# Block products of an MLP in another order with early weight differences, and a norm's row scale applied at the up projection's evacuation

## The chip, the cores and the metric

The kernel runs on one core of a Trainium2 chip. A core has a matrix engine (PE) and a vector engine (DVE), a scalar engine (ACT), a general engine (POOL) and an engine that issues most of the transfers (SP). Each runs its own list of instructions in order; they wait for one another by semaphores. The metric is the device time of one execution in microseconds. The kernel before took 896.69 us, the median of 3 runs (895.31 to 898.7).

## The reference, cut to what matters

One layer works on 512 tokens of width 1024: a mixer of recurrent heads, a cross-attention to 256 memory tokens, and a multilayer perceptron (MLP). The change touches the end of the second step and the whole third:

```python
x = x + cross_attention(rmsnorm(x, norm_xattn[l]), rmsnorm(mem, norm_mem[l]),
                        w_xq[l], w_xkv[l], w_xo[l])
x = x + squared_relu_mlp(rmsnorm(x, norm_mlp[l]), w_up[l], w_down[l])
return rmsnorm(x, norm_final)

def rmsnorm(x, g):
    y = x32 * lax.rsqrt(jnp.mean(x32 * x32, axis=-1, keepdims=True) + NORM_EPS)
    return y * g
def squared_relu_mlp(xn, w_up, w_down):
    return jnp.square(jax.nn.relu(xn @ w_up)) @ w_down
```

The factor 1/rms of a token is positive and the same for all of its columns. So relu(r·z) equals r·relu(z), and the factor can be applied before the up product or behind it.

## The kernel before, in words

**A product.** All products are of fp32 precision, made of three matmuls each: an operand is split into a rounded high part and the rest, and high·high, high·low and low·high are added in PSUM (`mm3`, L223 to L226). A weight tile of 128x1024 comes by a transfer into a buffer `st`, ACT rounds it to `wh` (L220), DVE subtracts to get `wl` (L221). There are three buffers each of `st`, `wh` and `wl`, and three weights are prepared ahead of the one in use.

**Stages.** The input projection and the recurrent heads come first (to about 390 us), then the mixer's output projection "out" with the residual addition, the query projection and the cross-attention, its output projection "xo", and from 545 us on the MLP. "out" and "xo" take the output columns in two halves c of 512, each with four tiles of 128 tokens. Behind "out" (`proj_res`) each finished piece is added to the residual, its squares are summed for the norm, and PE transposes it in four 128x128 pieces (`transp`, L768) while the next pieces are still in work; the norm's 1/rms goes into the attention later. Behind "xo" (`proj_res_norm`) nothing is transposed in the first half. In the second half, for each of the four tiles, the two sums of squares are added, POOL raises the mean to the power -1/2 (L166), DVE and ACT multiply the two halves of x by that factor (L788, L789), and only then PE transposes both: eight groups of four transposes, all behind the last matmuls of "xo".

**The MLP.** It has four blocks f of 1024 hidden columns. In a block, the *up stage* makes eight slices (p, j) of 128 hidden columns for all 512 tokens, 24 matmuls each. ACT evacuates a slice with Relu (L964) and squares it (L965); DVE and ACT then form the differences of token halves and split them. The *down stage* multiplies by the block's part of the down matrix with seven block products P1 to P7 in place of eight, each for the two halves g of the hidden columns: 14 jobs of 12 matmuls, 168 in all (L1006 to L1008). The products need differences of weight tiles, for which `source` (L891) issues four DVE subtractions per half g, 128x1024 each. The products gather in three pairs of PSUM banks: X takes P1, then P6, P7 and P4 on top of it; Y takes P2; Z takes P5, then P3. Whenever a bank holds a value that an output piece needs, `add_to` adds it to the residual on DVE (L938), and the next product may write into that bank only after. Behind the last block's adds come the final norm and the output transfers.

**Order.** The code is written stage by stage; a scheduler orders the instructions of each engine by priorities, and the preparation of weights has high priority. At run time each engine follows that order without exception, so what stands behind a waiting instruction waits too.

The jobs' order and the buffers before:

```python
G4 = lambda dt=F32: T("gate", 1024, 3, dt)      # three buffers of 128x1024
ORDER = ("P1", "P2", "P5", "P6", "P3", "P7", "P4")
JOBS = [("P1", 0), ("P2", 0), ("P1", 1), ("P2", 1)] + [(p, g) for p in ORDER[2:] for g in range(2)]
```

Of the kernel before, what the change touches and what calls it, by code (L numbers as in the profile page):

```python
# [18 lines left out]
P = 128  # L19
# [58 lines left out]
def trunk(ctx: ExitStack, tc: tile.TileContext, x, mem, wpk, vec, cst, lmask, rmask, rows, out):  # L78
# [12 lines left out]
    def T(tag, w, bufs, dt=F32):  # L91
        return (sb if w == 516 else big).tile([P, w], dt, tag=tag, name=nm(tag), bufs=bufs)
# [4 lines left out]
    def smb():  # L97
        return pss.tile([P, 512], F32, tag="sm", name=nm("sm"))
# [8 lines left out]
    A16 = lambda: T("as", 2560, 2)  # L107
    A4 = lambda dt=F32: T("a4", 1024, 10, dt)
    T2 = lambda: T("t2", 516, 5)
    G4 = lambda dt=F32: T("gate", 1024, 3, dt)  # L110
    VV = lambda: T("vv", 516, 8)
    XT = lambda: [T("xT", 4096, 2, F32R) for _ in range(2)]
    YT1 = lambda dt=F32R: T("yT", 1024, 8, dt)
# [7 lines left out]
    grow1 = G4()  # L121
# [532 lines left out]
    def gate_proj(c0, bcol, silu):  # L654
        gt = G4()
# [40 lines left out]
    rate[0] = 2  # L696
    mv_proj()
    rate[0] = 1
    mo0 = gate_proj(4096, V_MO, False)
    mo1 = gate_proj(4352, V_MO + 2, False)  # L700

    mt = [A4(), A4()]
# [57 lines left out]
                stats(st, t, c)  # L760
                transp(tgt, t, c)

    def transp(tgt, t, c, src=None):
        dst, gcol = tgt
        src = xr[t, c] if src is None else src
        ps = smb()
        for k in range(4):
            pe.transpose(ps[:, k * P:k * P + P], src[:, k * P:k * P + P], ident)  # L768
        for k in range(4):
            g = vc[:, gcol + 4 * c + k:gcol + 4 * c + k + 1]  # L770
            hi = dst[c][:, k * 1024 + t * P:k * 1024 + t * P + P]
            lo = dst[c][:, k * 1024 + 512 + t * P:k * 1024 + 512 + t * P + P]
            sc.activation(hi, ps[:, k * P:k * P + P], AF.Copy, scale=g)
            v.scalar_tensor_tensor(out=lo, in0=ps[:, k * P:k * P + P], scalar=g, in1=hi.bitcast(F32), op0=ALU.mult, op1=ALU.subtract)  # L774

    def proj_res_norm(mat, src, tgt, st, pre):

        for c in range(2):
            for t, ps in proj_t(mat, 0, 512 * c, src, pre=pre if c == 0 else None, late=c == 1):
                v.tensor_tensor(out=xr[t, c], in0=ps, in1=xr[t, c], op=ALU.add)  # L780
                stats(st, t, c)
                if c == 0:
                    continue
                s1 = tiny(1)
                v.tensor_tensor(out=s1, in0=st[:, 2 * t:2 * t + 1], in1=st[:, 2 * t + 1:2 * t + 2], op=ALU.add)
                r, _ = rstd_of(s1, 1, D)
                n0, n1 = T2()[:, 0:512], T2()[:, 0:512]
                v.tensor_scalar(out=n0, in0=xr[t, 0], scalar1=r, scalar2=None, op0=ALU.mult)  # L788
                sc.activation(n1, xr[t, 1], AF.Copy, scale=r)  # L789
                transp(tgt, t, 0, n0)  # L790
                transp(tgt, t, 1, n1)

    def rstd_tok(st, n=1.0):
        s4 = tiny(4)
# [94 lines left out]
    def source(f, p, g):  # L889
        b11, b12, b21, b22 = [raw[f, 4 * g + n] for n in range(4)]  # L890
        sub = lambda o, a, b: v.tensor_tensor(out=o, in0=a, in1=b, op=ALU.subtract)  # L891
# [59 lines left out]
    for f in range(4):  # L951

        sta = []
        for p in range(4):
            a = []
            for j in range(2):
                ps, = proj_d("up", 1024 * f + P * (p + 4 * j), x3, count=1)
                raw_load(f, 2 * p + j)
                if p == 3 and j == 1:
                    with tc.high_priority():  # L960
                        job(f, 0)
                        job(f, 1)
                y = T2()[:, 0:512]
                sc.activation(y, ps, AF.Relu)  # L964
                sc.activation(y, y, AF.Square)  # L965
                a.append(y)
            if p % 2 == 0:
# [19 lines left out]
            e["P5"], e["P6"] = [(ya[:, u:u + 256], ya[:, 512 + u:768 + u]) for u in (0, 256)]  # L987
            e["P7"], e["P3"] = [(yb[:, u:u + 256], yb[:, 512 + u:768 + u]) for u in (0, 256)]
            sta.append(e)
        fin = f == 3  # L990
        if fin:
            gfin = G4()
# [131 lines left out]
```

## Time and profile before

| what | value |
|---|---|
| median of 3 runs | 896.69 us |
| profiled execution | 896.54 us |
| its span, first to last instruction | 894.8 us |
| mean granted PE clock | 0.991 of full |
| PE busy | 860.9 us, 96% |
| DVE busy | 592.4 us, 66% |
| ACT busy | 434.3 us, 49% |
| up stage of a block (629.40 to 672.90 us) | 43.5 us |
| down stage of a block (588.50 to 629.40 us) | 40.9 us |
| last down stage (841.98 to 886.37 us) | 44.4 us |

All times in the prediction are microseconds from the span's start. In the rows of a timeline stand the start, the duration, the engine, the line and the operation, output and inputs, and in brackets the idle time just before and what ended it. Matmuls overlap: one of 128x512 is listed with 0.39 us, and the next starts 0.227 us after it, so a distance between starts says more than a duration. In a table of windows each engine has its busy time and, in brackets, its instructions, and at the end stand the granted PE clock (1.00 is full), the share of the transfer engines and GB/s.

### The profile page before, as it was taken

The page shows a single profiled execution, that of the slowest core. Times are in us where ns is not written, and L with a number is a line of the kernel's source. Part 1 is how long each engine was busy: PE and PEld are TensorE (multiplying, and loading weights), DVE is VectorE, ACT ScalarE, POOL GpSimd, SP SyncE. Part 2 cuts the span into 40 slices and gives each one's busy share as a digit, 9 for nine tenths or more (in the row PEclk, how much of TensorE's full clock was granted, in tenths as well). Part 3 has the DMA queues.
Part 4 walks back from the last instruction along what each step waited for, and adds up shares of the span by engine and source line. Part 5 has one row for each costly group of instructions (what it writes and reads, how often), then busy time and mean ns, then how long its engine had stood idle before and what let it go on. Part 6 is the DMA issues. An engine that isn't in the chain of part 4 may idle for free.

```text
span 894.8 us, 11089 instructions
## 1 busy us (share of the span) xinstructions
PE 860.9 (96%) x4194; PEld 711.5 (80%) x4194; DVE 592.4 (66%) x1016; ACT 434.3 (49%) x793; POOL 20.4 (2%) x53
## 2 busy tenths in 40 slices
PE   7999999999999999999999998999999999999985
PEld 5887888888876987887888876887887788778864
DVE  5557688689346977654555455688568746955785
ACT  5235443353358567454445355553554356436534
POOL 1000000010010000000000000000000000000000
PEclk9999999999999999999999998999999999999998
DMA  7422222221142333522222422403330432052002
GB/s 255 133 101 73 75 82 77 96 78 54 48 141 71 99 126 107 166 93 94 71 67 76 143 70 71 142 24 117 118 118 25 141 118 94 24 188 95 1 1 94
DMA packets 24615, 84.21 MB, mean 94 GB/s; under 512 B 2865, under 2 KB 2993, under 8 KB 24562
## 3 DMA queue, kind: packets, MB, share of 16 engines
q1 hardware_dynamic: 24272, 83.04, 27.3%
q8 instruction: 33, 0.54, 0.3%
q10 hardware_dynamic: 290, 0.47, 0.2%
q14 instruction: 20, 0.16, 0.1%
HBM read 81.40 MB, written 2.10 MB: 93 GB/s over the span
## 4 chain that ended last, share of the span: by engine, by line
PE 54%; DVE 11%; ACT 3%; issue 2%; POOL 1%; POOLq 0%; ACTq 0%
PE mm L225 13%; PE mm L224 13%; PE mm L226 13%; DVE wl L221 5%; PE sm L1006 2%; PE sm L1007 2%; PE sm L1008 2%; ACT wh L220 2%; PE sm L628 2%; PE sm L613 2%; DVE a L891 2%; DVE vv L938 1%; PE sm L226 1%; PE sm L225 1%; PE sm L224 1%
## 5 line engine op out<-in xcount | busy, mean ns | idle before, releaser
L221 DVE TENSOR_TENSOR wl<-st,wh 128x1024 fp32r<-128x1024 f32 x109 | 133.4, 1224 | 154.1 <-ACT wh L220 150.7
L224 PE MATMUL mm<-xT,wh 128*128 128x512 f32 x552 | 219.6, 399 | 0.1
L225 PE MATMUL mm<-xT,wh 128*128 128x512 f32 x552 | 215.9, 392 | 0.2 <-DVE xT L774 0.2
L226 PE MATMUL mm<-xT,wl 128*128 128x512 f32 x552 | 216.0, 392 | 0.0
L220 ACT ACTIVATE wh<-st 128x1024 fp32r<-128x1024 f32 x109 | 115.3, 1058 | 182.1 <-PE mm L225 83.7
L226 PEld LDWEIGHTS mm<-xT,wl 128*128 128x128 f32 x552 | 103.7, 188 | 22.2 <-issue 0.6
L224 PEld LDWEIGHTS mm<-xT,wh 128*128 128x128 f32 x552 | 103.8, 188 | 21.7 <-issue 1.4
L225 PEld LDWEIGHTS mm<-xT,wh 128*128 128x128 f32 x552 | 103.9, 188 | 21.3 <-DVE xT L774 0.8
L1006 PE MATMUL sm<-wh,yT 128*128 128x512 f32 x128 | 50.3, 398 | 5.4 <-DVE vv L938 5.4
L1007 PE MATMUL sm<-wl,yT 128*128 128x512 f32 x128 | 51.1, 399 | 1.5 <-DVE wl L221 1.5
L224 PE MATMUL mm<-wh,yT 128*128 128x512 f32 x128 | 50.4, 394 | 0.0
L226 PE MATMUL mm<-wh,yT 128*128 128x512 f32 x128 | 50.3, 393 | 0.0
L225 PE MATMUL mm<-wl,yT 128*128 128x512 f32 x128 | 50.0, 391 | 0.0
L1008 PE MATMUL sm<-wh,yT 128*128 128x512 f32 x128 | 48.9, 394 | 0.0
L220 ACT ACTIVATE wh<-as 128x1024 fp32r<-128x1024 f32 x24 | 25.5, 1061 | 40.7 <-PE mm L225 21.4
L221 DVE TENSOR_TENSOR wl<-as,wh 128x1024 fp32r<-128x1024 f32 x24 | 29.4, 1224 | 16.1 <-ACT wh L220 16.1
L938 DVE TENSOR_TENSOR vv<-sm,vv 128x512 f32<-128x512 f32 x48 | 31.7, 685 | 6.4 <-PE sm L1008 6.4
L1006 PEld LDWEIGHTS sm<-wh,yT 128*128 128x128 f32 x128 | 24.3, 190 | 12.0 <-issue 4.3
L220 ACT ACTIVATE wh<-a 128x1024 fp32r<-128x1024 f32 x20 | 20.8, 1058 | 23.6 <-PE sm L1008 23.3
L375 PEld LDWEIGHTS sm<-a,t 128*128 128x128 f32 x224 | 30.2, 192 | 2.2 <-ACT t L365 0.4
L365 ACT ACTIVATE t<-a 128x512 f32<-128x512 f32 x28 | 18.4, 673 | 26.3 <-DVE a L428 24.0
L166 POOL TENSOR_TENSOR tiny<-tiny,misc 128x1 f32<-128x1 f32 (+1 forms) x22 | 16.4, 747 | 641.3 <-DVE tiny L947 334.5
(264 smaller groups left out, 1590.3 us busy)
## 6 DMA issues: line engine op xcount, KB each, us to landing
st<-in_wpk SPq DMA_DIRECT2D x109, 512.0 KB, 3.2
as<-in_wpk SPq DMA_DIRECT2D x16, 512.0 KB, 4.1
gate<-in_wpk SPq DMA_DIRECT2D x8, 512.0 KB, 3.3
a<-in_wpk SPq DMA_DIRECT2D x8, 512.0 KB, 5.1
as<-in_x SPq DMA_DIRECT2D x4, 512.0 KB, 6.4
vv<-in_x SPq DMA_DIRECT2D x8, 256.0 KB, 4.0
out<-vv SPq DMA_DIRECT2D x7, 256.0 KB, 2.2
a<-in_mem SPq DMA_DIRECT2D x2, 512.0 KB, 4.0
```

What stands on the lines that cost most here:

```text
L220: sc.activation(dst_hi, src, AF.Copy)
L221: v.tensor_tensor(out=dst_lo, in0=src, in1=dst_hi.bitcast(F32), op=ALU.subtract)
L224: pe.matmul(ps, lhsT=ah, rhs=bh, start=first, stop=False)
L225: pe.matmul(ps, lhsT=ah, rhs=bl, start=False, stop=False)
L226: pe.matmul(ps, lhsT=al, rhs=bh, start=False, stop=last)
L365: sc.activation(t[:, 0:512].rearrange("p (b e j) -> p b e j", e=2, j=L), ap(k, 0, [2 * L, 512 // (2 * L)], [512 + L, 2], [1, L]), AF.Copy)
L375: pe.matmul(ps[:, z], lhsT=kc[:, z], rhs=ap(q2, w * P, [2 * L, P // (2 * L)], [512 + L, 2], [1, L]), start=True, stop=True)
L613: pe.matmul(ps, lhsT=k[:, ws * P:ws * P + P], rhs=q, start=True, stop=True)
L938: v.tensor_tensor(out=z, in0=ps, in1=z, op=ALU.add)
L1006: pe.matmul(ps, lhsT=ah, rhs=bh, start=new, stop=False, **fl)
L1007: pe.matmul(ps, lhsT=ah, rhs=bl, start=False, stop=False, **fl)
L1008: pe.matmul(ps, lhsT=al, rhs=bh, start=False, stop=end and k == 1, **fl)
```

## The change

There are three parts.

1. **The norm behind "xo".** `proj_res_norm` goes; "xo" uses `proj_res` as "out" does, so that the unscaled x is transposed piece by piece. The factor 1/rms of all 512 tokens is computed once, on 128x4 numbers. PE turns it into a row (four transposes of a column spread over 128 columns, `rms_row`), and ACT copies it to `rrow`, which holds each token's factor in every partition. Each up slice's evacuation multiplies by it: ACT's Relu becomes a DVE instruction, max(ps, 0)·rrow (L964), and ACT squares as before.
2. **The products.** ORDER becomes P1, P2, P6, P5, P7, P3, P4. The differences b22-b12 and T2 = b22-b12+b11 are formed in `early_sums`, called behind the second and the fourth pair of up slices; P6 then takes T2 and P7 takes b12 as they are, and P5 and P4 keep one subtraction each. The number of subtractions stays at eight per block. The raw down weights are requested in the first six slices of a block's up stage, two at once in the first two, where before one was requested in each of the eight.
3. **Buffers.** The three `gate` buffers become two and one named `rg` of the same size, which holds in turn a gain row, a gate, `rrow` and the final gain row.

```diff
-    G4 = lambda dt=F32: T("gate", 1024, 3, dt)
+    G4 = lambda dt=F32: T("gate", 1024, 2, dt)
+    RG = lambda: T("rg", 1024, 1)
...
-    proj_res_norm("xo", os_, (x3T, V_MLP), st2, drain)
+    proj_res("xo", 0, os_, (x3T, V_MLP), st2, drain)
     x3 = xk(x3T)
+    ms2 = rstd_tok(st2)
+    r4 = tiny(4)
+    gp.tensor_tensor(out=r4, in0=ms2, in1=nh.to_broadcast([P, 4]), op=ALU.pow)
+    rrow = RG()
+
+    def rms_row():
+        ps = smb()
+        for t in range(4):
+            pe.transpose(ps[:, t * P:t * P + P], r4[:, t:t + 1].to_broadcast([P, P]), ident)
+        sc.activation(rrow[:, 0:512], ps, AF.Copy)
...
-    ORDER = ("P1", "P2", "P5", "P6", "P3", "P7", "P4")
+    ORDER = ("P1", "P2", "P6", "P5", "P7", "P3", "P4")
...
         if p == "P5":
-            sub(b11, b12, b11)
+            sub(b11, b22, raw[f, g, "T2"])
             return b11
         if p == "P6":
-            t2 = raw[f, g, "T2"] = A4()[:, :]
-            sub(t2, b22, b11)
-            return t2
+            return raw[f, g, "T2"]
         if p == "P7":
-            sub(b12, b22, b12)
             return b12
         sub(b21, b21, raw[f, g, "T2"])
         return b21
+
+    def early_sums(f, g):
+
+        b11, b12, b21, b22 = [raw[f, 4 * g + n] for n in range(4)]
+        v.tensor_tensor(out=b12, in0=b22, in1=b12, op=ALU.subtract)
+        t2 = raw[f, g, "T2"] = A4()[:, :]
+        v.tensor_tensor(out=t2, in0=b12, in1=b11, op=ALU.add)
...
                 ps, = proj_d("up", 1024 * f + P * (p + 4 * j), x3, count=1)
-                raw_load(f, 2 * p + j)
+                for n in ((0, 1), (2, 3), (4,), (5,), (6,), (7,), (), ())[2 * p + j]:
+                    raw_load(f, n)
...
+                if f == 0 and p == 0 and j == 0:
+                    rms_row()
                 y = T2()[:, 0:512]
-                sc.activation(y, ps, AF.Relu)
+                v.scalar_tensor_tensor(out=y, in0=ps, scalar=0.0, in1=rrow[:, 0:512], op0=ALU.max, op1=ALU.mult)
                 sc.activation(y, y, AF.Square)
...
+            if p % 2 == 1:
+                early_sums(f, p // 2)
```

How the instructions of three places now stand is shown below. In these rows a tile's name carries a number that tells its copies apart.

**The end of "xo" on PE.** `mm` with `yT` is the last product of "xo", `sm` out of `cs` is a group of transposes, `mm` with `xT` is an up slice. Before:

```order
L226 MATMUL mm_4347<-wh_4378,yT_4257 128x512
L768 MATMUL sm_4547<-cs,t_787_4543 128x128 x4
L768 MATMUL sm_4560<-cs,t_788_4544 128x128 x4
L768 MATMUL sm_4598<-cs,t_795_4594 128x128 x4
L768 MATMUL sm_4611<-cs,t_796_4595 128x128 x4
L224 MATMUL mm_4630<-xT_4126,wh_4408 128x512
```

With the change:

```order
L226 MATMUL mm_4399<-wl_4431,yT_4257 128x512
L768 MATMUL sm_4549<-cs,vv_3225 128x128 x4
L227 MATMUL mm_4399<-wh_4430,yT_4257 128x512
L225 MATMUL mm_4597<-xT_4126,wh_4460 128x512
L226 MATMUL mm_4597<-xT_4126,wh_4460 128x512
L227 MATMUL mm_4597<-xT_4126,wl_4461 128x512
L225 MATMUL mm_4597<-xT_4126,wh_4460 128x512
L768 MATMUL sm_4571<-cs,vv_3227 128x128 x4
L226 MATMUL mm_4597<-xT_4126,wh_4460 128x512
```

The transposes now read the residual `vv` and not a scaled copy `t`, and the last two groups lie among matmuls; the four row transposes (L861) come some 20 matmuls later, inside the first up slices.

**The start of a down stage on DVE** (block 0). `vv<-sm` at L938 is the first add out of the banks X, which P1 filled. L891 are the weight differences. Before:

```order
L221 TENSOR_TENSOR wl_4981<-gate_4832,wh_4980 128x1024
L891 TENSOR_TENSOR a_878_5050<-as_4744,as_4655 128x1024
L891 TENSOR_TENSOR gate_4832<-gate_4866,gate_4832 128x1024
L891 TENSOR_TENSOR as_4744<-as_4744,a_878_5050 128x1024
L891 TENSOR_TENSOR a_881_5068<-a_853_4944,gate_4832 128x1024
L891 TENSOR_TENSOR gate_4866<-a_853_4944,gate_4866 128x1024
L221 TENSOR_TENSOR wl_4997<-a_850_4914,wh_4996 128x1024
L221 TENSOR_TENSOR wl_5014<-as_4655,wh_5013 128x1024
L891 TENSOR_TENSOR a_850_4914<-a_850_4914,a_881_5068 128x1024
```

With the change (L906 and L884 are differences, L935 is the add):

```order
L222 TENSOR_TENSOR wl_4976<-a_824_4812,wh_4975 128x1024
L222 TENSOR_TENSOR yT_4944<-t_846_4938,yT_4944 128x512
L222 TENSOR_TENSOR yT_4945<-t_847_4939,yT_4945 128x512
L906 TENSOR_TENSOR a_850_4951<-gate_4756,gate_4720 128x1024
L222 TENSOR_TENSOR wl_4992<-a_819_4779,wh_4991 128x1024
L884 TENSOR_TENSOR gate_4720<-a_829_4846,a_850_4951 128x1024
L884 TENSOR_TENSOR a_824_4812<-a_824_4812,a_850_4951 128x1024
L222 TENSOR_TENSOR wl_5010<-a_850_4951,wh_5009 128x1024
L935 TENSOR_TENSOR vv_3213<-sm_4953,vv_3213 128x512
```

Of a block's eight differences six stood between `wl` of the second P1 job (`wl_4981`) and the first add, and two ahead of it in the up stage. With the change three stand between the same two instructions (`wl_4960` is that job's there, some rows above those shown), and five in the up stage.

**The step from the second product to the third on PE** (block 0). `mm` at L1008 to L1010 is P2, `sm` with `yT` a later product. Before, the first matmuls of P5 went into the banks Z ahead of most of P2:

```order
L1008 MATMUL sm_4975<-wh_4980,a_843_4871 128x512
L1006 MATMUL mm_4976<-wh_4996,a_844_4874 128x512
L1006 MATMUL mm_4977<-wh_4996,a_844_4874 128x512
L1006 MATMUL sm_4978<-wh_5013,yT_4707 128x512
L1006 MATMUL sm_4979<-wh_5013,yT_4707 128x512
L1007 MATMUL mm_4976<-wl_4997,a_844_4874 128x512
```

With the change:

```order
L1009 MATMUL mm_4956<-wl_4976,a_845_4935 128x512
L1010 MATMUL mm_4956<-wh_4975,a_845_4935 128x512
L1008 MATMUL sm_4957<-wh_5028,yT_4683 128x512
L1008 MATMUL sm_4958<-wh_5028,yT_4683 128x512
L1008 MATMUL sm_4953<-wh_4991,yT_4683 128x512
L1009 MATMUL sm_4953<-wl_4992,yT_4683 128x512
```

`sm_4957` and `sm_4958` are the banks Z, into which two matmuls of P5 go ahead of P6; `sm_4953` is a bank X that P1 filled and the first add must have read before P6 (`wh_4991`) writes on top. With three buffers `wh_5028`, the third weight behind `wh_4975` (`wh_4991` and `wh_5009` are between), takes the buffer that the second P2 job uses until its last matmul.

More of the change, by code (lines that the diff above doesn't have):

```diff
@@ L120, in trunk @@
     ident = cs[:, C_ID:C_ID + P]
-    grow1 = G4()
+    grow1 = RG()
     xin = [A16(), A16()]
@@ L652, in hgrn_proj, with gate_proj @@
                 hgrn_evac(p, which, [(j, ps)], hst)
-    def gate_proj(c0, bcol, silu):
-        gt = G4()
+    def gate_proj(c0, bcol, silu, buf=G4):
+        gt = buf()
         for j, ps in enumerate(proj_d("in", c0, xs)):
@@ L698, in trunk @@
     rate[0] = 1
-    mo0 = gate_proj(4096, V_MO, False)
+    mo0 = gate_proj(4096, V_MO, False, RG)
     mo1 = gate_proj(4352, V_MO + 2, False)
@@ L761, in proj_res, with transp @@
                 transp(tgt, t, c)
-    def transp(tgt, t, c, src=None):
+    def transp(tgt, t, c):
         dst, gcol = tgt
-        src = xr[t, c] if src is None else src
         ps = smb()
         for k in range(4):
-            pe.transpose(ps[:, k * P:k * P + P], src[:, k * P:k * P + P], ident)
+            pe.transpose(ps[:, k * P:k * P + P], xr[t, c][:, k * P:k * P + P], ident)
         for k in range(4):
@@ L774, in transp @@
             v.scalar_tensor_tensor(out=lo, in0=ps[:, k * P:k * P + P], scalar=g, in1=hi.bitcast(F32), op0=ALU.mult, op1=ALU.subtract)
[L776 to L791, printed above, removed]
     def rstd_tok(st, n=1.0):
@@ L989, in trunk @@
             sta.append(e)
+            if p % 2 == 1:
+                early_sums(f, p // 2)
         fin = f == 3
         if fin:
-            gfin = G4()
+            gfin = RG()
             nc.sync.dma_start(out=gfin, in_=rows[3:4, :].to_broadcast([P, D]))
```

## The prediction

> **What bounds the kernel now.** First the page's busy times, then what the matrix engine waits for, then a table by stage.
>
> ```profile
> PE 860.9 (96%) x4194; PEld 711.5 (80%) x4194; DVE 592.4 (66%) x1016; ACT 434.3 (49%) x793; POOL 20.4 (2%) x53
> ```
> ```profile
> PE sm L1006 <- DVE vv L938: 7.3, 8, 2.2
> PE sm L768 <- DVE t L788: 6.2, 3, 5.2
> PE sm L1007 <- DVE wl L221: 1.5, 4, 0.4
> ```
> ```profile
> 588.50:629.40 40.90, 39.10 (x169) 31.27 (x168) 33.23 (x40) 17.62 (x19) 0.00 (x0) 1.00 0.26 91
> 629.40:672.90 43.50, 43.50 (x193) 36.03 (x193) 25.32 (x37) 23.22 (x35) 0.00 (x0) 1.00 0.32 109
> 841.98:886.37 44.39, 40.97 (x169) 32.25 (x167) 36.40 (x50) 21.47 (x33) 1.25 (x3) 0.96 0.06 24
> 536.00:540.00 4.00, 0.00 (x0) 0.00 (x0) 3.10 (x8) 1.52 (x4) 0.42 (x1) 0.68 0.52 156
> 540.00:545.00 5.00, 3.73 (x17) 3.10 (x18) 2.58 (x9) 3.88 (x11) 0.68 (x2) 0.57 0.25 88
> 868.00:872.00 4.00, 4.00 (x13) 3.13 (x12) 1.86 (x4) 0.00 (x0) 0.00 (x0) 0.57 0.02 4
> 68.00:72.00 4.00, 2.34 (x13) 1.93 (x13) 3.95 (x5) 2.18 (x4) 0.00 (x0) 1.00 0.00 0
> ```
>
> PE is the bound: 96% busy, so a gain can only come from its waits, from stretches at a lower clock, or from the tail. The waits list (total, times, longest) names the places: the transposes behind "xo" wait 6.2 us for the scaled copies (L788), the down products 7.3 us for adds (L938) and 1.5 us for a weight's low part. The change removes no matmul. An up stage is full: 192 matmuls in 43.50 us, 0.2266 apart. A down stage has 168; at that pace they take 38.1 us, and the first window shows 40.90: **2.8 us are lost in each**, in the last one 6.1 (its last matmul starts at 885.98, row below, so 44.23 less 38.1). The waits listed are less than that (11 rows and 8.8 us for four blocks), since idle counts only from a matmul's modelled end. So I count from start to start. The clock fell twice in this part, in the windows at 536 and 540 and at 868, to 0.57.
>
> **Term 1, the end of "xo".** On PE:
>
> ```profile
> 526.87 0.39 PE L226 MATMUL mm<-wh,yT 128*128 128x512 f32 x1
> 535.07 0.39 PE L226 MATMUL mm<-wh,yT 128*128 128x512 f32 x1
> 540.70 1.97 PE L768 MATMUL sm<-cs,t 128*128 128x128 f32 x8 [5.25 <-DVE t L788]
> 544.85 0.96 PE L224 MATMUL mm<-xT,wh 128*128 128x512 f32 x3
> ```
> ```profile
> 414.69 0.48 PE L226 MATMUL mm<-wh,yT 128*128 128x512 f32 x1
> 415.01 0.60 PE L768 MATMUL sm<-cs,vv 128*128 128x128 f32 x4
> 415.37 0.47 PE L224 MATMUL mm<-wh,yT 128*128 128x512 f32 x1
> 424.14 0.51 PE L225 MATMUL mm<-xT,wh 128*128 128x512 f32 x1 [0.22 <-DVE xT L774]
> ```
>
> From 526.87 to 544.85 are 17.98 us. In them lie 25 matmuls (5.67) and the eight groups of four transposes (two halves of four token tiles), half of them behind the last matmul. The second fence is the same place behind "out", where unscaled pieces are transposed between matmuls: from 414.69 to 415.37 a matmul and a group take 0.68, so a group costs 0.45, eight 3.6. That leaves 17.98 - 9.27 = 8.7 us of waiting and of half clock. With the change "xo" runs the code that "out" runs, and the step from "out" to the query projection is what it becomes: there the one wait is the 0.22 before 424.14. New on PE are four row transposes, by the same rows 0.45. For the refill behind a wait I take 0.1. The gain is 8.7 - 0.22 - 0.45 - 0.1 = **7.9 us**. At best nothing waits, 8.25.
>
> The row transposes wait for POOL's power, and PE in order with them, with the whole first up slice queued behind. The same chain behind "out":
>
> ```profile
> 422.05 0.16 DVE L797 TENSOR_SCALAR tiny<-tiny 128x4 f32<-128x4 f32 x1
> 422.29 1.01 POOL L806 TENSOR_TENSOR misc<-tiny,misc 128x4 f32<-128x4 f32 x1 [52.74 <-DVE tiny L797]
> 417.96 0.40 PE L224 MATMUL mm<-xT,wh 128*128 128x512 f32 x1
> ```
>
> POOL was done at 423.30. The row transposes lie some 22 matmuls (5.0) and a group (0.45) behind the first up matmul, 417.96 here: 423.4. So there it just suffices; rival C is that it doesn't. The slice's evacuation then waits for the row's copy too, but a slice's bank is needed again only slices later, 5.4 us each.
>
> **The evacuation's new engine.** ACT loses 32 Relus, DVE gains 32 three-operand instructions out of PSUM:
>
> ```profile
> L964 ACT ACTIVATE t<-mm 128x512 f32<-128x512 f32 x32 | 18.5, 577 | 0.0
> L450 DVE SCALAR_TENSOR_TENSOR gate<-sm,vc,gate 128x512 f32<-128x512 f32 x8 | 6.0, 747 | 2.1 <-PE sm L449 2.1
> 590.71 1.22 DVE L891 TENSOR_TENSOR a<-as,as 128x1024 f32<-128x1024 f32 x1
> 591.85 1.22 DVE L891 TENSOR_TENSOR gate<-gate,gate 128x1024 f32<-128x1024 f32 x1
> 606.41 0.68 DVE L938 TENSOR_TENSOR vv<-sm,vv 128x512 f32<-128x512 f32 x1
> 607.01 0.68 DVE L221 TENSOR_TENSOR yT<-t,yT 128x512 fp32r<-128x512 f32 x1
> 601.53 0.42 DVE L980 TENSOR_TENSOR t<-t,t 128x256 f32<-128x256 f32 x1
> 601.86 0.42 DVE L982 TENSOR_TENSOR t<-t 128x256 f32<-128x256 f32 x1
> ```
>
> L450 is the nearest row: 0.75. From start to start a DVE instruction of 1024 columns takes 1.135, one of 512 0.60 and one of 256 0.33. An up stage's DVE work was 25.3 of 43.5; three more differences there (3.4) and eight evacuations (at 0.60 to 0.75) bring it to 34 or 35. So PE stays the bound, and its 8.5 us of slack hide the term: nothing for 0.60, nothing for 0.75. The cover is gone from 1.85 an evacuation on (43.5 - 28.7, over eight); that is rival D.
>
> **Term 2, the down stages.** What waited in block 0:
>
> ```profile
> 588.50 0.39 PE L1006 MATMUL sm<-wh,a 128*128 128x512 f32 x1
> 612.39 0.47 PE L1006 MATMUL sm<-wh,yT 128*128 128x512 f32 x1 [1.05 <-DVE vv L938]
> 623.89 0.47 PE L1006 MATMUL sm<-wh,a 128*128 128x512 f32 x1 [0.38 <-DVE vv L938]
> ```
>
> The first is the step into P3 (72 matmuls are left), the second the step into P4 (24 are left). Before, P7 and P4 both wrote X, one right behind the other, so P4 waited for P7's add (0.38). In the new order P1, P2, P6, P5, P7, P3, P4 another product of 24 matmuls (5.4 us) always lies between two that write the same banks, so this wait goes. P3 had that cover before too; its 1.05, and the 0.4 for a low part ahead of it, came from DVE, which was behind with the differences (33.23 of 40.90 busy, most of it early). Three of those are now done in the up stage, so I take these two as gone. What stays is the first step, P2 to P6, where DVE is still full. I go through DVE's order with time t from the first P1 matmul. From t = 1.07 (ACT's 1.06 for the second P1 weight; a row shows 1.06 throughout, below) DVE does seven instructions of 1024 columns (four low parts, three differences: 7.95), three of 512 (1.80) and four of 256 (1.34), 11.09 in all, and then the first add, from 12.17 to 12.85. PE goes on some 0.15 later, at 13.0.
>
> ```profile
> L220 ACT ACTIVATE wh<-a 128x1024 fp32r<-128x1024 f32 x20 | 20.8, 1058 | 23.6 <-PE sm L1008 23.3
> ```
>
> PE has its 48 matmuls of P1 and P2 behind it at 10.88. Two of P5 follow in its order, which need a `wh` whose buffer P2's last matmul has just freed: ACT from 11.07 to 12.13. So PE waits 1.27 for ACT, does the two (0.45, to 12.6) and waits 0.4 for the add: **1.66 us of new wait**. Behind it DVE has caught up: the second X add ends at 14.5, and PE reaches that bank eight matmuls after 13.0, at 14.8. A stage becomes 38.1 + 1.66 + 0.2 for two refills = 39.95, for 40.9 before: about 1.0 each, **3.0 us in three**. Bounds for the wait: 0 if DVE gets ahead, 2.6 if a 1024 instruction costs its full 1.22 (0.6 more) and the evacuation of the last slice comes 0.3 later; then a stage gains nothing.
>
> The raw weights are requested up to 11 us earlier, in an up stage that uses 0.32 of the transfer engines. SP's queue gets them ahead of two up weights, each of which is wanted slices later. Their buffers come free as P7, P5, P3 and P4 are split, in the last 10 us of a down stage, ahead of their first use, so I cost them at nothing; the first difference of a block stands on DVE ahead of the next up weights' low parts, and would hold those if a transfer of the usual length came late:
>
> ```profile
> as<-in_wpk SPq DMA_DIRECT2D x16, 512.0 KB, 4.1
> ```
>
> 4.1 us behind a split at t = 33 is 37, and the low part is wanted at 45 or so.
>
> **Term 3, the last block and the tail.**
>
> ```profile
> 867.08 0.47 PE L1006 MATMUL sm<-wh,yT 128*128 128x512 f32 x1 [2.24 <-DVE vv L938]
> 885.98 0.39 PE L1008 MATMUL sm<-wh,a 128*128 128x512 f32 x1
> 884.25 0.68 DVE L938 TENSOR_TENSOR vv<-sm,vv 128x512 f32<-128x512 f32 x1
> 887.47 0.68 DVE L938 TENSOR_TENSOR vv<-sm,vv 128x512 f32<-128x512 f32 x1
> ```
>
> Here the norm's work makes the adds later, and the wait before P3 was 2.24, after which the clock was 0.57 for some 3.4 us. Both go; the stage takes 39.95 where 44.23 were, 4.3 less. But in the new order P3 and P4 end it, and the adds of P3's banks finish two tokens' norms just ahead of P4's adds. Such a chain (add, squares, power, scaling) takes DVE 3.22 us, by the two adds at 884.25 and 887.47; two token tiles queue there, and by their instructions the last add starts 2.4 us behind PE's end, where it was 1.1 (887.47 for 886.37). That gives back 1.3. The rest of the tail stays. **3.0 us** net.
>
> **Sum.** The profiled execution took 896.54, its span 894.8 and 1.74 around it; the median shown is 896.69, the same within 0.02%. 896.54 - 7.9 - 3.0 - 3.0 = **882.6 us**.
>
> **The clock.** After 5.25 and 2.24 of idle the clock fell; after 1.66 it did not:
>
> ```profile
> 69.69 0.43 PE L553 MATMUL sm<-cs,a 64*128 64x64 f32 x4 [1.66 <-DVE a L542]
> ```
>
> (the window at 68 shows 1.00). The new idle is 1.27 and 0.4 with two matmuls between, below both, so I cost no drop. The Trainium skill's page "TensorE: Matmul & The Clock Gate", section "Why this matters for your kernels", puts the bound at gaps over about 3 us; the trace has a drop after 2.24, so the bound is lower here, and by the page's rule no clock is lost either.
>
> **The rivals.**
> A. The new wait doesn't come, because the scheduler's order lets DVE run ahead. For it: DVE has 8 us of slack in an up stage. Against: its last part depends on the last slice. 4 x 1.66 less: 876.0.
> B. The clock halves after the new wait, in every block. For: 1.27 + 0.4 is only just below the 1.66 that did no harm. Against: that row. Half speed for 3.4 us costs 1.7, so 4 x 1.7 = 6.8: 889.4.
> C. PE waits for the row transposes, in place of the scaled copies, as long as 5.25: 887.9. For: the chain's 423.30 against 423.4 has no reserve. Against: the chain is a fraction of the old one.
> D. The slower side: DVE becomes the bound of the up stages. It decides from 1.85 us an evacuation on; at 2.4, eight of them overrun by 4.4 us a stage and 17.6 in four, and the time is 900. For: PSUM is read and a third operand added. Against: L450 shows 0.75.
> E. The wait behind "xo" merely moves to the up product, which now needs the low parts from DVE, and term 1 gives 1 or 2 us: about 889. Against: the 0.22 behind "out". If, beyond that, the down stages gain nothing either, it is 894.
>
> **How the numbers follow.** Forecast 0.62, A 0.10, B 0.12, C 0.06, D 0.04, E 0.06. The range leaves out A, D and the end of E, and reaches B: 877.5 to 890.5. What can be told from no change begins at 0.5%, 4.5 us: faster is below 892.2. That holds for the forecast, A, B, C and half of E (0.93); I keep back 0.04 for an unseen wait. So 0.89 faster, 0.07 the same, 0.04 slower.
>
> **What would show it.** Term 1: no wait of over 0.3 us at L768 or L861, no stretch at 0.57 around 540. Term 2: one wait of about 1.3 for ACT and one of 0.4 for the add between P2 and P6 in each block, and none before P3 and P4; down stages of 40.0. Term 3: no 2.24 wait, the last add 2.4 behind PE's last matmul. DVE's busy time rises by some 22 (32 x 0.68), ACT's falls by 18.5, the span is 880.9. Wrong would be: up stages over 43.6 (D), a clock under 1.00 inside the blocks (B), waits elsewhere in the down stages.

## The result, and the profile after

The changed kernel takes **882.17 us** (median of 4 runs, 881.93 to 884.17) against 896.15 us (median of 4, 895.31 to 898.7): a ratio of 0.9844, 95% interval 0.9819 to 0.9869. The forecast was 882.6, with a range of 877.5 to 890.5. The profiled execution took 882.23, its span is 880.4 us. Among the experiments below, one execution of "DVE load late" took 924.88 us at a mean granted clock of 0.896, where its other six took 890.09 to 893.65 at 0.987 to 0.992; the kernel's median counts it, the ratio does not. The page of the changed kernel opens with the busy times:

```profile
PE 855.4 (97%) x4198; PEld 709.1 (81%) x4198; DVE 609.7 (69%) x1038; ACT 415.2 (47%) x758; POOL 19.2 (2%) x50
```

DVE has 17 us more and ACT 19 us less. PE's waits (total, times, longest), as far as they belong to this part of the kernel:

```profile
PE sm L1008 <- ACT wh L221: 4.8, 4, 1.2
...
PE mm L226 <- DVE xT L774: 0.2, 1, 0.2
```

The 6.2 us at the transposes (L768), the 7.3 us for adds and the 1.5 us for low parts are gone from the list. One new wait stands there, four times 1.2 us, once a block. The end of "xo" on PE:

```profile
535.28 0.60 PE L768 MATMUL sm<-cs,vv 128*128 128x128 f32 x4
535.63 0.48 PE L227 MATMUL mm<-wh,yT 128*128 128x512 f32 x1
535.95 0.39 PE L225 MATMUL mm<-xT,wh 128*128 128x512 f32 x1
536.90 0.66 PE L768 MATMUL sm<-cs,vv 128*128 128x128 f32 x4
541.26 0.39 PE L225 MATMUL mm<-xT,wh 128*128 128x512 f32 x1
541.49 0.27 PE L861 MATMUL sm<-cs,tiny 128*128 128x128 f32 x1
541.51 0.47 PE L226 MATMUL mm<-xT,wh 128*128 128x512 f32 x1
580.50 0.39 PE L1008 MATMUL sm<-wh,a 128*128 128x512 f32 x1
```

The transposes lie between matmuls, the first row transpose (L861) follows the matmul before it at the usual distance of 0.23, and the first P1 matmul starts at 580.50 where it was 588.50. The step from P2 to the third product in block 0, on PE, on ACT and on DVE:

```profile
591.16 0.39 PE L1010 MATMUL mm<-wh,a 128*128 128x512 f32 x1
592.75 1.17 PE L1008 MATMUL sm<-wh,yT 128*128 128x512 f32 x3 [1.21 <-ACT wh L221]
593.76 0.40 PE L1009 MATMUL sm<-wl,yT 128*128 128x512 f32 x1
```
```profile
591.64 1.06 ACT L221 ACTIVATE wh<-as 128x1024 fp32r<-128x1024 f32 x1 [1.72 <-PE mm L1010]
```
```profile
590.40 1.22 DVE L884 TENSOR_TENSOR a<-a,a 128x1024 f32<-128x1024 f32 x1
591.54 1.22 DVE L222 TENSOR_TENSOR wl<-a,wh 128x1024 fp32r<-128x1024 f32 x1
592.67 0.69 DVE L935 TENSOR_TENSOR vv<-sm,vv 128x512 f32<-128x512 f32 x1
```

ACT has the weight ready at 592.70, and PE does the two matmuls of P5. The third matmul of that row is the first of P6; by the row's end it starts at about 593.5, behind the add's end at 593.36. So of the two waits the add's ends last, though the list names ACT. The first add runs from 12.17 to 12.86 us after 580.50, and PE goes on at about 13.0, as worked out in the prediction. The windows of a down stage, an up stage and the last down stage (busy time of PE, PEld, DVE, ACT, POOL with their instructions, then the clock):

```profile
580.50:620.34 39.84, 38.63 (x170) 31.38 (x168) 31.82 (x39) 17.03 (x18) 0.00 (x0) 1.00 0.27 92
620.34:663.86 43.52, 43.52 (x194) 36.05 (x192) 31.69 (x46) 19.55 (x29) 0.00 (x0) 1.00 0.33 110
830.57:870.56 39.99, 38.78 (x169) 31.19 (x167) 33.94 (x46) 20.22 (x30) 1.12 (x2) 1.00 0.08 27
```

The down stage took 39.84 us where it took 40.94, the clock is 1.00 in all of them, and the up stage is as long as before though DVE now has 31.7 us of work in it.

The new evacuation is in the page's groups, 0.69 us each (busy, mean ns, idle before):

```profile
L964 DVE SCALAR_TENSOR_TENSOR t<-mm,rg 128x512 f32<-128x512 f32 x32 | 22.1, 690 | 38.3 <-PE mm L227 38.3
```

### The profile page after: what moved, and what is told of

It reads as the page before. It is cut to its first block, busy times and chain, and to the rows that moved or that the text cites. A ratio compares the mean times of both kernels' runs of the same rounds, so it can differ in the third digit from the quotient of the medians.

```text
span 880.4 us, 11056 instructions
## 1 busy us (share of the span) xinstructions
PE 855.4 (97%) x4198; PEld 709.1 (81%) x4198; DVE 609.7 (69%) x1038; ACT 415.2 (47%) x758; POOL 19.2 (2%) x50
## 4 chain that ended last, share of the span: by engine, by line
PE 65%; DVE 2%; ACT 1%; POOL 0%; issue 0%; POOLq 0%; ACTq 0%
PE mm L226 14%; PE mm L227 14%; PE mm L225 14%; PE sm L1008 5%; PE sm L1009 5%; PE sm L1010 5%; PE sm L629 2%; PE sm L614 2%; ACT wh L221 1%; PE mm L1010 1%; PE mm L1009 1%; PE mm L1008 1%; PE sm L768 1%; PE sm L227 1%; PE sm L226 1%; PE sm L225 1%
## 5 line engine op out<-in xcount | busy, mean ns | idle before, releaser
L1008 PE MATMUL sm<-wh,yT 128*128 128x512 f32 x128 | 49.9, 397 | 4.8 <-ACT wh L221 4.8
L1010 PE MATMUL sm<-wh,yT 128*128 128x512 f32 x128 | 49.2, 389 | 0.0
L964 DVE SCALAR_TENSOR_TENSOR t<-mm,rg 128x512 f32<-128x512 f32 x32 | 22.1, 690 | 38.3 <-PE mm L227 38.3
L935 DVE TENSOR_TENSOR vv<-sm,vv 128x512 f32<-128x512 f32 x48 | 31.9, 684 | 4.8 <-PE sm L1010 4.7
L1008 PEld LDWEIGHTS sm<-wh,yT 128*128 128x128 f32 x128 | 23.7, 188 | 12.6 <-ACT wh L221 6.5
L222 DVE TENSOR_TENSOR wl<-a,wh 128x1024 fp32r<-128x1024 f32 x20 | 24.4, 1222 | 11.1 <-ACT wh L221 11.1
```

What stands on the lines that cost most here:

```text
L222: v.tensor_tensor(out=dst_lo, in0=src, in1=dst_hi.bitcast(F32), op=ALU.subtract)
L935: v.tensor_tensor(out=z, in0=ps, in1=z, op=ALU.add)
L964: v.scalar_tensor_tensor(out=y, in0=ps, scalar=0.0, in1=rrow[:, 0:512], op0=ALU.max, op1=ALU.mult)
L1008: pe.matmul(ps, lhsT=ah, rhs=bh, start=new, stop=False, **fl)
L1010: pe.matmul(ps, lhsT=al, rhs=bh, start=False, stop=end and k == 1, **fl)
```

## The experiments

The table gives what each kernel took and, from its trace, the start of the first P1 matmul and the lengths of the four down stages from start to start (the last one to the start of its last matmul). All up stages but the first took 43.5 us in every kernel.

| kernel | median us | ratio to before, 95% interval | first P1 at | down stages |
|---|---|---|---|---|
| before | 896.15 | | 588.50 | 40.94, 40.97, 41.01, 44.00 |
| the change | 882.17 | 0.9844 (0.9819 to 0.9869) | 580.50 | 39.84, 39.82, 39.84, 39.60 |
| the norm alone | 887.93 | 0.9908 (0.9884 to 0.9933) | 581.40 | 41.03, 40.99, 41.02, 42.24 |
| the products alone | 890.05 | 0.9936 (0.9916 to 0.9956) | 588.76 | 39.74, 39.70, 39.71, 39.51 |
| late differences | 901.37 | 1.0060 (1.0039 to 1.0081) | 580.50 | 43.81, 44.05, 45.04, 44.86 |
| old order | 876.85 | 0.9788 (0.9770 to 0.9807) | 580.33 | 38.74, 38.75, 38.75, 38.97 |
| first adds ahead | 879.19 | 0.9807 (0.9788 to 0.9826) | 581.84 | 39.12, 39.14, 39.13, 38.91 |
| first adds and differences ahead | 875.94 | 0.9767 (0.9747 to 0.9786) | 580.04 | 38.08, 38.08, 38.08, 37.86 |
| DVE load early | 881.73 | 0.9837 (0.9814 to 0.9860) | 580.20 | 39.82, 39.81, 39.83, 39.58 |
| DVE load late | 893.12 | 0.9949 (0.9932 to 0.9966) | 581.97 | 42.52, 42.52, 40.92, 42.32 |
| old order, P7 by halves | 874.36 | 0.9742 (0.9728 to 0.9757) | 580.37 | 38.08, 38.08, 38.08, 38.96 |
| differences alone | 885.74 | 0.9864 (0.9847 to 0.9880) | 590.77 | 38.75, 38.75, 38.75, 39.08 |

Each ratio is to runs of the kernel before on the same chip, whose medians lay between 895.44 and 897.94; so between kernels that ran on different chips the ratios and the stages say more than the medians. The position of a kernel's first P1 matmul varies by some 2 us, mostly with its early part, which no experiment's edit touched, so a difference of one or two microseconds is read from the stages. Counted from one and the same matmul of "xo" (the first of its last 156, at 497.18 before and at 497.12 with the change), the first P1 matmul comes after 83.37 to 83.42 us in all nine kernels that have the norm's change, and after 91.32, 91.88 and 92.47 us in the three without it (before, the products alone, the differences alone).

**The norm alone.** Old order, old differences, old weight requests; the rest of the change stays.

```diff
-    ORDER = ("P1", "P2", "P6", "P5", "P7", "P3", "P4")
+    ORDER = ("P1", "P2", "P5", "P6", "P3", "P7", "P4")
...
-            if p % 2 == 1:
-                early_sums(f, p // 2)
```

> Only the norm's part of the change (unscaled transposes behind "xo", 1/rms as a row at the up slices' evacuation); order of the products, differences and weight requests as before. Theory (the parts add, each at its own place): the first P1 matmul comes 8.0 us earlier as in the changed kernel, the down stages keep their lost time of 2.8 us or lose some tenths more, since DVE's list at their start is as full as before: 888 to 891 us, about 889. Rival 1 (the evacuation on DVE costs time that only the early differences give back): 893 or more. Rival 2 (the row's gain is worth only what the interleaved transposes save, without the clock): 892.

Measured: 887.93, with P1 7.1 us earlier than before (7.9 counted from "xo") and the first three down stages as before, within 0.1 us. The last one was 1.8 shorter, since it waited as long as before and the clock did not fall (below). Rivals 1 and 2 fall: neither does the evacuation cost a down stage anything, nor is the gain at "xo" much smaller than thought.

**The products alone.** The other half: order, differences and weight requests of the change, norm and Relu of before.

```diff
-    proj_res("xo", 0, os_, (x3T, V_MLP), st2, drain)
+    proj_res_norm("xo", os_, (x3T, V_MLP), st2, drain)
...
-                v.scalar_tensor_tensor(out=y, in0=ps, scalar=0.0, in1=rrow[:, 0:512], op0=ALU.max, op1=ALU.mult)
+                sc.activation(y, ps, AF.Relu)
```

> Only the products' part (new order, early differences, earlier weight requests); the norm behind "xo" and ACT's Relu as before. Theory: the 8.0 us at "xo" are missing, the down stages and the tail give their 6 to 6.5 us: about 890, with the 5.25 us wait at the scaled transposes back. Rival (the two parts need each other, because Relu on ACT makes the last slice late): 893 or more, with the wait at the step from P2 to P6 over 2.5 us.

Measured: 890.05. The transposes have their 5.2 us wait back, and the down stages are 39.7, 0.1 shorter than in the whole change. The wait between P2 and P6 is there too, with another engine's name beside it:

```profile
599.42 0.39 PE L1015 MATMUL mm<-wh,a 128*128 128x512 f32 x1
601.18 0.47 PE L1013 MATMUL sm<-wh,yT 128*128 128x512 f32 x1 [1.37 <-DVE vv L942]
```

Here PE's order has no matmul of P5 ahead of P6, and PE waits for the add itself. So with no wait for ACT's weight at that step the stage is still only 0.1 shorter, which parts the add from ACT. The two halves gain 7.5 and 5.4 us beside the same runs of the kernel before, 12.9 in all; the whole gains 14.0 beside runs of its own. In ratios the halves gain 0.92% and 0.64%, together the 1.56% of the whole.

**Late differences.** The changed kernel, with T2 and its difference formed where P6 is prepared.

```diff
         if p == "P6":
+            early_sums(f, g)
             return raw[f, g, "T2"]
...
-            if p % 2 == 1:
-                early_sums(f, p // 2)
```

> The changed kernel with the new order, but the two differences of T2 formed only when P6 is prepared, not in the up stage. Theory (DVE's full list at the start of a down stage sets the wait; every difference there costs 1.135 us): by DVE's order the first add comes at 14.0 us after the first P1 matmul instead of 12.2 and the last split for P2 at 13.0, a loss of 3.8 us a block instead of 1.7: about 890.5, up to 897 if the clock falls after such waits. Rival (the new order alone brings the gain in the down stages, since it puts a product between any two that write the same banks): 882 to 884.

Measured: 901.37, slower than the kernel before. The rival, that the order brings the gain, is out by more than 17 us. The theory's loss of 3.8 us is there, and more: block 0's stage shows it (43.81 less 38.08 is 5.7). The rows of PE and the window just behind:

```profile
593.67 0.73 PE L1009 MATMUL mm<-wh,a 128*128 128x512 f32 x2 [1.87 <-DVE a L222]
595.56 1.22 PE L1007 MATMUL sm<-wh,yT 128*128 128x512 f32 x2 [1.15 <-ACT wh L221]
596.58 0.63 PE L1008 MATMUL sm<-wl,yT 128*128 128x512 f32 x1
597.00 0.63 PE L1009 MATMUL sm<-wh,yT 128*128 128x512 f32 x1
```
```profile
595.00:599.00 4.00, 3.44 (x9) 2.78 (x10) 4.00 (x7) 1.55 (x3) 0.00 (x0) 0.57 0.00 0
```

Matmuls start 0.42 apart there, and the clock is 0.57: it fell in the blocks, which I had named as the upper end (897). The measured time lies 4 us above that end; the stages show it (44 to 45 us, where 3.8 of wait and 1.7 of slow clock on 38.1 would make 43.6). In the last two blocks the clock stayed low for 6.8 us, twice as long as costed (769.3 to 776.1 and 858.0 to 864.9).

**Old order.** The changed kernel with the products in the order of before, and nothing else.

```diff
-    ORDER = ("P1", "P2", "P6", "P5", "P7", "P3", "P4")
+    ORDER = ("P1", "P2", "P5", "P6", "P3", "P7", "P4")
```

> The changed kernel with early differences, but the products in the order of before (P1, P2, P5, P6, P3, P7, P4). Theory (what mattered is DVE's relief; the new order itself brings the 1.7 us wait, because P6 writes on P1's banks 5.4 us after them, where P5 writes into fresh ones): no wait behind P2, about 0.6 us where P4 follows P7, the last add 1.1 behind PE's end again: 876 to 878, faster than the change. Rival (the new order is what gains): 885 to 888, with waits ahead of P3 and P4 as before.

Measured: 876.85, 5.3 us less than the change. The new order costs time: 1.1 us in each of three stages, 0.6 in the last, and the rest in the tail, where the last add starts 1.1 us behind PE's end (2.5 with the change). With the early differences, the old order has one short wait a block, at the step from P7 to P4, and none behind P2:

```profile
613.51 0.47 PE L1008 MATMUL sm<-wh,a 128*128 128x512 f32 x1 [0.38 <-DVE vv L935]
```

**First adds ahead.** The changed kernel, with P1's adds alone at high priority in the scheduler.

```diff
-        v.tensor_tensor(out=z, in0=ps, in1=z, op=ALU.add)
+        with (tc.high_priority() if early else ExitStack()):
+            v.tensor_tensor(out=z, in0=ps, in1=z, op=ALU.add)
```

> The changed kernel, with P1's adds alone at high priority: on DVE they now stand ahead of three weight differences and two splits, and nothing else is removed. Theory (DVE's list ahead of the first add sets the new wait, ACT's share of it comes only from PE's order): the add ends at 8.3 us after the first P1 matmul instead of 12.85; what is left is the buffer of one P5 weight and the late split of P6, about 0.8 to 1.0 us a block for 1.74, so 878 to 880. Rival (ACT's rounding of the P5 weight is the wait, as the list of waits names it): 882 as the change.

Measured: 879.19, stages of 39.13, 0.7 less a block. The first add ends 8.3 us after the first P1 matmul, as expected. What moved is DVE's order, and with it PE's; ACT's work and buffers are the same. PE's wait for ACT fell from 1.2 to 0.5 since two matmuls of P6 can now go ahead of P5's; what the list still shows is for ACT:

```profile
PE sm L1009 <- ACT wh L221: 2.1, 4, 0.5
```

**First adds and differences ahead.** In addition the second half's differences go one pair of slices earlier.

```diff
-            if p % 2 == 1:
-                early_sums(f, p // 2)
+            if p == 1:
+                early_sums(f, 0)
+            if p == 2:
+                early_sums(f, 1)
```

> The changed kernel in its new order, with P1's adds at high priority and the second half's T2 formed one pair of slices earlier, so that DVE's list ahead of the first add is 3 to 4 us shorter and PE's order goes from P2 straight into P6. Theory: no wait at that step, down stages of 38.1 to 38.3 us, 875 to 876. Rival (P6 on P1's banks costs something whatever DVE does, as in the clock or in the banks): 879 or more.

Measured: 875.94, stages of 38.08: 168 matmuls at 0.2267 and nothing else. So in these stages the new order has no cost of its own once DVE is not in the way. Its longer tail stays: the last add starts 2.5 us behind PE's end here too. PE's order moved along with DVE's (P5's matmuls no longer stand ahead of P6), so this run by itself does not say which of the two took the last 1.05 us; that the add held PE in the changed kernel rests on its rows and on the products alone.

**DVE load early and late.** Added instructions of 128x512 on DVE, whose result is not used: in the first run three behind each of the first four slices of a block, in the second two behind the last slice.

```diff
                 sc.activation(y, y, AF.Square)
+                for _ in range(3 if p < 2 else 0):              # the run "early"
+                for _ in range(2 if (p, j) == (3, 1) else 0):   # the run "late"
+                    v.tensor_tensor(out=rrow[:, 512:1024], in0=y, in1=rrow[:, 0:512], op=ALU.mult)
```

> The changed kernel with 12 more DVE instructions of 128x512 in each block, three behind each of the first four up slices (their result is not used): 7.2 us of DVE work a block, by which the up stage's 31.4 us become 38.6 of 43.5. Theory (PE bounds the up stage and DVE's evacuation is hidden there): 882 to 883, no change. Rival (evacuating on DVE costs PE something already, or a late evacuation holds a bank): 2 us a block or more, 890 or more.

> The changed kernel with only 2 more DVE instructions of 128x512 in each block, behind the last up slice (their result is not used): 1.2 us a block where DVE's list is full. Theory (the time from the last slice to the first add is DVE's, so a sixth of the work of the run with 12 costs more than that whole run): 0.8 to 1.2 us a block, 885.5 to 887. Rival (the wait there is ACT's): no change, 882.

Measured: 881.73 and 893.12. Twelve instructions a block in the first half of an up stage change nothing. The window of an up stage with them (DVE is the third engine):

```profile
620.02:663.54 43.52, 43.52 (x194) 36.05 (x192) 38.46 (x58) 19.19 (x29) 0.00 (x0) 1.00 0.32 110
```

DVE is busy for 38.46 of 43.52 us, and PE as full as before. Two instructions at the end cost 1.08 us a block by the one stage in which the clock stayed at 1.00 (40.92 less 39.84), as the theory said, and 2.7 in the three in which it fell. The total is 6 us over the expected range: the three falls make 4.8 of it, and in the profiled execution the first P1 matmul came 1.5 later. The rival, a wait of ACT's, is out.

**Old order, P7 by halves.** Both weights of P7 for its first bank, then both for the second, as P4 has it.

```diff
-            if p == "P4":
-                ws = [ahead(n), ahead(n + 1)]
+            if p in ("P7", "P4"):
+                ws = [ahead(n), ahead(n + 1) if p == "P4" else job(f, n + 1)]
...
-                    add_to(2 + u, 0, bank[p][u], fin)
+                    add_to(2 + u, int(p == "P7"), bank[p][u], fin)
```

> The changed kernel with the products in the order of before, and P7 done by token halves as P4 is: both weight halves for its first bank, then both for the second. So 12 matmuls instead of 6 lie between P7's last write to a bank and P4's first. Theory: the 0.65 us that is left in each down stage with the old order goes, stages of 38.1 to 38.2 us, the tail stays as with the old order: 874 to 875, the shortest so far. Rival (holding both of P7's weights delays P4's second weight by one buffer): a wait at P4's second half, 876 to 878.

Measured: **874.36**, 7.8 us below the change and 0.9742 of the kernel before: the shortest of all. The first three down stages take 38.08, the matmuls alone; the last one keeps a wait of 0.7 us for a low part (38.96). The window of block 0's:

```profile
580.37:618.45 38.08, 38.08 (x170) 31.53 (x168) 31.73 (x39) 17.02 (x18) 0.00 (x0) 1.00 0.27 95
```

**Differences alone.** The kernel before with the early differences and weight requests only; order, norm and Relu as before.

```diff
-                raw_load(f, 2 * p + j)
+                for n in ((0, 1), (2, 3), (4,), (5,), (6,), (7,), (), ())[2 * p + j]:
+                    raw_load(f, n)
...
+            if p % 2 == 1:
+                early_sums(f, p // 2)
```

> The kernel before with nothing but the early differences and the earlier weight requests: old order, old norm, Relu on ACT. Theory (the early differences alone give the down stages' gain, without the row norm and the new order): stages of 38.8 us, 2.2 less than before in three and 5 in the last, 883 to 885. Rival (they need DVE's evacuation, since ACT's Relu makes the last slice later): stages of 40 us, 888 to 890.

Measured: 885.74, 0.7 above the range, with stages of 38.75 as in the run with the old order. In its profiled execution (887.19, the longest of its four) the first P1 matmul stood 2.3 us later than in the one of before. Of these, 1.1 stand already at the matmul of "xo" named above; the rest lies behind the wait at the transposes, after which the clock stayed low until 548.4 (before: 544.3). The early differences, with the earlier requests that they need, therefore bring the whole gain of the down stages and more: 2.2 us a stage, where the change has 1.1. The requests without the early differences, as in the late differences, do not.

## Why the prediction was right

- **What bounds the kernel.** PE, counted from start to start. The experiments' floor confirms the measure: a down stage without waits takes 38.08 (forecast 38.1), and an up stage 43.52 in every kernel, with DVE at 25 or at 38 us. One count is off: the list of waits before has 12 waits in the four blocks (8 and 4), not 11; no sum uses it.
- **Term 1, 7.9 us.** The first P1 matmul came 8.0 us earlier. The one wait of 0.22 before the second half of x is there (0.2 in the list), the row transposes start at 541.49 right behind a matmul, and the clock around 540 is 1.00. Counted from "xo" on, the way to the first P1 matmul is 7.9 us shorter (83.38 for 91.32), and just as much with the norm alone (83.40).
- **The evacuation at nothing.** 32 instructions of 0.69 us each (between the 0.60 and 0.75 taken), and no change of an up stage. DVE's busy time was forecast too high, 34 or 35 us in an up stage and 22 more in all, and came out at 31.69 and 17 more; by the counts (46 instructions there for 37, where eleven were added) some of its work moved out of the up stage. The term does not depend on it: twelve more instructions a block change nothing either. In the run with the late load, though, the cover that the prediction named ends with the last slice: what DVE does from there to the first add is paid in full.
- **Term 2, 3.0 us in three stages.** 3.4: stages of 39.84 for the forecast 39.95. The first add at 12.17 us and the wait were where they had been put. The forecast split the new wait into 1.27 for ACT and 0.4 for the add, and the list shows the one for ACT. The cause is DVE's list: the add's end is what P6 waits for in the changed kernel's rows and in the products alone, where no wait for ACT lies beside it. Moving the adds up in the list takes 0.7 of the 1.76 lost, moving the differences as well takes all of it, with PE's order moving along in both.
- **Term 3, 3.0 us.** The last down stage is 4.4 shorter (forecast 4.3) and the tail 1.4 longer (forecast 1.3). Some 1.8 of the 4.4 is the fall of the clock in the profile before, which the same wait did not bring in the norm alone; so the size of this term hung on the profile that it was read from. The end of the changed kernel on DVE:

```profile
869.86 0.68 DVE L935 TENSOR_TENSOR vv<-sm,vv 128x512 f32<-128x512 f32 x1
...
873.08 0.68 DVE L935 TENSOR_TENSOR vv<-sm,vv 128x512 f32<-128x512 f32 x1
```

PE's last matmul ends at 870.56, so the last add starts 2.5 us behind it (forecast 2.4, before 1.1); between the two adds lies one token's norm, 3.22 us, as before.
- **The rivals.** A (the wait doesn't come) was put at 876.0: the run that removes it, first adds and differences ahead, took 875.94. B (the clock falls behind the new wait) did not happen in the changed kernel, but it nearly does: 1.2 us more of DVE work at that place and it falls in three blocks of four. C, D and E did not come.
- **The clock: the right result, in part by luck.** The prediction took from one row that 1.66 us of idle do no harm. The same wait, 1.67 to 1.69 us at the same place, stands in the profiles of all other kernels here, and in four of them the clock fell right behind it (norm alone, first adds ahead, DVE load late, differences alone: 0.57 to 0.64 from 70 to 74 us). The length of a wait was the wrong measure; the last section shows one that fits, and by it the changed kernel's waits had a margin that the prediction had not worked out.
- **What the prediction did not see.** It read the new order as a gain: always a product between two that write the same banks. The runs show the reverse. Beside the early differences it costs 1.1 us net a block (39.84 for 38.75): it puts P6, which writes on P1's banks, where P5 had fresh banks, just when DVE is full, and the 0.6 us that it saves at P4 is less than that; it also makes the tail 1.4 longer. The sum was right because the new order had been worked through with DVE's list as it stands, but no term was made for the order alone, and so the rival that the differences do better without it was missing.

## What to carry to other kernels

Where a chain of products reuses banks, what counts is not only how many matmuls lie between two writes, but what the evacuating engine has queued ahead of the add in that time; go through its list instruction by instruction. An engine with idle time on average can be full for 11 us where it matters: moving work out of that stretch was worth 2.2 us a block here, and the same work in the stage before cost nothing. When a change has several parts, cost each of them alone: here the new order of the products worked against the norm's part and the early differences.

## What the runs showed of the hardware that I had not expected

The clock's fall does not follow from the length of a wait alone. In the kernel before, 2.24 us of idle in the last block were followed by a clock of 0.57. In the run with the norm alone the same place waited as long, and the clock stayed:

```profile
860.07 0.47 PE L1001 MATMUL sm<-wh,yT 128*128 128x512 f32 x1 [2.23 <-DVE vv L931]
```
```profile
858.00:862.00 4.00, 1.93 (x9) 1.63 (x10) 4.00 (x6) 1.29 (x3) 0.00 (x0) 1.00 0.00 0
862.00:866.00 4.00, 4.00 (x19) 3.34 (x18) 2.41 (x4) 1.89 (x4) 0.00 (x0) 1.00 0.02 4
```

And in the run with the late load, the four blocks have the same two waits, as its list shows:

```profile
PE sm L1010 <- ACT wh L221: 4.8, 4, 1.2
PE sm L1011 <- DVE wl L222: 4.3, 4, 1.1
```

But the clock fell in three of the blocks only. The windows of 10 us around the step in the four blocks:

```profile
590.00:600.00 10.00, 7.73 (x27) 5.65 (x26) 8.96 (x11) 2.12 (x2) 0.00 (x0) 0.84 0.00 0
676.00:686.00 10.00, 7.73 (x26) 5.64 (x25) 9.00 (x11) 2.12 (x2) 0.00 (x0) 0.83 0.01 2
762.00:772.00 10.00, 7.73 (x33) 5.79 (x32) 9.03 (x11) 2.12 (x2) 0.00 (x0) 1.00 0.00 1
847.00:857.00 10.00, 7.74 (x27) 5.60 (x26) 9.78 (x13) 3.31 (x6) 0.00 (x0) 0.83 0.00 0
```

The same PE work, and a clock of 0.84, 0.83, 1.00 and 0.83; each fall costs 1.6 us (42.52 less 40.92). The runs of this kernel lie at about 890.2, 892.0 and 893.4, in steps of that size, as if their number of falls differed.

What decides can be read from the traces. In this profile the clock fell or came back at 71.16, 74.57, 596.81, 600.21, 682.11, 685.56, 852.81 and 856.21 us. All of these lie whole multiples of 3.413 us apart, to within 0.05 us: 230 steps from the first to the last. The other six profiles in which the clock fell ahead of the tail fit the same step, each from a start of its own. So here the clock changes on a fixed grid of 3.41 us. These are the stretches of the grid that hold most of the two waits, one in each block:

```profile
593.40:596.81 3.41, 1.53 (x5) 0.97 (x6) 3.41 (x5) 0.76 (x1) 0.00 (x0) 1.00 0.00 0
678.73:682.14 3.41, 1.14 (x5) 0.38 (x3) 3.41 (x5) 1.06 (x1) 0.00 (x0) 1.00 0.00 0
764.07:767.48 3.41, 1.75 (x7) 0.81 (x5) 3.41 (x4) 1.06 (x1) 0.00 (x0) 1.00 0.00 0
849.40:852.81 3.41, 1.15 (x4) 0.58 (x4) 3.41 (x5) 1.06 (x1) 0.00 (x0) 1.00 0.00 0
```

The first number in brackets is PE's matmuls: 5, 5 and 4 in the stretches ahead of the three falls, and 7 in block 2, where the waits run on into the next stretch. A full stretch holds 15. The other cases agree. The last block before had 6 ahead of its fall, the norm alone 8 and no fall, the late differences 3, 6, 6 and 5 ahead of their four falls. So in these stages the clock fell behind a stretch with 6 matmuls or fewer and held from 7 on, and the same wait may do harm or not by where it lies on the grid. The changed kernel's waits leave 9 or more in any 3.41 us around its steps from P2 to P6, wherever the grid lies, which explains why the clock held in its blocks. No run moved the grid on purpose.

The Trainium skill's page "TensorE: Matmul & The Clock Gate", section "Why this matters for your kernels", speaks of an idle window that brings the clock to half, with gaps over about 3 us as the ones to avoid. Here less was enough: one gap of 2.24 us, and two waits of 1.2 and 1.1 us within one stretch of 3.4 us.
